# Moving loads, stores and PSUM copies in a two-layer recurrent trunk (GLA, S5, mLSTM) on one core

## The chip, the cores and the metric

The kernel runs on one core of one Trainium2 chip. The metric is the device time of one execution in microseconds (us); lower is better. The time before is the median of three runs.

## What is computed

One inference step of a two-layer trunk, for a prompt of 256 tokens and for 8 samples of 8 tokens each (320 tokens, d_model 2048). Each of four sub-layers applies RMSNorm, a shift and scale from the condition vector (adaLN), its mixer or its SwiGLU feed-forward, and a gated residual add:

```python
def gla_mix(...):      # layer 0, 4 heads: S_t = diag(a_t) S_{t-1} + k_t^T v_t,  o_t = q_t S_t
def s5_mix(...):       # layer 0, 64 groups of 16 channels, each a 64-dim complex diagonal state (associative scan)
def mlstm_mix(...):    # layer 1, 4 heads: C_t = f_t C_{t-1} + i_t v_t k_t^T, n_t likewise, m_t a running maximum
...
x = x + gate * mixer(modulate(x, c, ...));  x = x + gate * swiglu(modulate(x, c, ...))
```

The outputs are the normed tokens of both groups and the final states: of GLA (128 x 256 for each head and sample), of S5, and of mLSTM (C of 512 x 256 for each head and sample, 512 KB; n; m).

## The kernel before

All large products are y = W^T x with the weights as the stationary operand in 128 x 128 tiles and the 320 tokens as the moving columns. Full precision comes from splitting both operands into a rounded part and a rest (`hi`, `lo` of the weights, `xh`, `xl` of the activations) and adding three products. Weights come in units of 512 KB on SyncE's (SP's) queue; ScalarE (ACT) makes `hi` by a cast, VectorE (DVE) makes `lo` by a subtraction, six half units ahead of the products (`split_to`, L590; `run_pair`, L604).

All else runs as generators (tasks) between these products. The kernel is written out once, in the order of a planner (`Est`, L130): a cost model with one clock for each engine, for SP and for the DMA engines. A task yields the tensors that it needs next; after every three products `tick` (L383) resumes the tasks whose tensors the model believes ready. What comes out is one fixed order of instructions for each engine, so an edit of a task shifts the order of all that comes after it. Each engine runs its own instructions in order, waiting on semaphores, and two engines that read the same PSUM bank wait for each other. When nothing else is ready, a filler product is emitted (`warm`, L389) or a step of the adaLN products (`ada`), which fill in between.

The order of the stages: conditions and first norm; input projection, with S5 and GLA as tasks; output projection; feed-forward 0; mLSTM projections with `ml_task`; output projection; feed-forward 1; last norm and output.

The places that the change touches:

- S5, `apply1` (L1178): for each of 8 blocks and each of two parts (`ri`), products into one bank, then a copy of 64 x 4 columns by ScalarE and one of 16 x 4 columns by VectorE out of that bank.
- S5, `toep` (L1297): for each of 8 blocks, 16 copies of 32 partitions out of one bank, in four groups (`i`) of four (`t`). The groups alternate between VectorE and ScalarE. `apply2` (L1310) multiplies by what they write.
- GLA, `gla_tail` (L1645), one for each head: a sample's new state is the product of masked keys `KM` (96 x 128) with values, and a DVE update of `S`. `km(b)` (L1664) makes the masked keys on GpSimd (POOL); the loop yields once for each of the 8 samples.
- mLSTM, `ml_gates` (L1933): the gate rows of all four heads in partitions 0 to 3 of `rows_b` (`Mr`, `er`, `gi`). At its end it loads the state n (`nr`), waits for it, transposes it and sets the flag "gates", for which `ml_task` waits.
- mLSTM, `ml_task` (L2066): for each head three products spread a row of `rows_b` over all 128 partitions (L2093 to L2100, below); `sel` is 1 in row h and 0 in all other rows. Then, for each of 8 samples (step g = 8 h + b), C lies in one of three buffers `CR`. The order of a step is: yield for C and for `EV`; `old(b - 1)`; `store(g - 1)` on SP; eight transposes of C; yield; products; two DVE updates of C in place; `load_c(g + 2)` on SP, into the buffer that `store(g - 1)` reads.
- `ml_begin` (L2292) opens the stage's memory and loads the constants. `z1_end` (L2337) waits for the flag "nout", which `ml_task` sets at its end, before the output projection begins.

```python
mm(ps[:, 0:T], sel[0:4, h, :], ML["er"])
act.copy(eb, ps[:, 0:T])
mm(ps[:, T:T + 64], sel[0:4, h, :], ML["gi"])
act.copy(gb, ps[:, T:T + 64])
```

In the profile every instruction has the line of one helper (L220), so instructions are told apart by their tiles: `misc` are the small PSUM banks, `mm` the large ones, `ada` the adaLN bank; `S_slab`, `G_slab`, `GR_slab` and `R_slab` are the memories of S5, GLA, GLA's masked keys and mLSTM; `fix_slab` holds weights and constants.

Of the kernel before, what the change touches and what calls it, by code (L numbers as in the profile page):

```python
# [16 lines left out]
AF = mybir.ActivationFunctionType  # L17
# [216 lines left out]
def trunk(tc, a, o, coff, dbg=None, stop=None):  # L234
# [5 lines left out]
    with (  # L240
# [66 lines left out]
        def con(name):  # L307
            f, n = coff[name]
            return cst[0].v(n, o=f) if f < NC1 else cst[1].v(n, o=f - NC1)
# [30 lines left out]
        def f(ap):  # L340
            return ap.bitcast(F32)
# [786 lines left out]
        def s5_task():  # L1128
# [49 lines left out]
            def apply1(j):  # L1178
                U4 = U4_b.v(4, 81, o=324 * (j % 3))
                M1 = M1_b[j % 2].v(8, P)  # L1180
                pr4 = slice(4 * j, 4 * j + 4)
                for ri in range(2):
                    ps = mps()
                    for i in range(4):
                        mm(ps[:, 81 * i:81 * i + 81], M1[:, 4 * ri + i, :], U4[:, i, :])
                    pv = ps[:, 0:324].rearrange("p (q c) -> p c q", q=4)
                    act.copy(H[:, 1:65, ri, pr4], pv[:, 0:64, :])
                    vec.tensor_copy(H[:, 73:89, ri, pr4], pv[:, 65:81, :])

            done1, done2 = [0, 0], [0, 0]  # L1190
            build1(0)
# [105 lines left out]
            def toep(j):  # L1297
                WBf, TT = WB_b.v(2, 4, 160, o=1280 * (j % 2)), TT_b.v(4, P, o=512 * (j % 2))
                ps = yield from kept()
                for ri in range(2):  # L1300
                    for i in range(4):
                        mm(ps[32 * i:32 * i + 32, 0:P], BB[:, ri, i, :], WBf[:, ri, i, 0:P], ri == 0, ri == 1)
                yield [ps]
                for i in range(4):
                    for t in range(4):
                        (act.copy if i % 2 else vec.tensor_copy)(TT[32 * t:32 * t + 32, i, 32 * t:P],
                                                                 ps[32 * i:32 * i + 32, 0:P - 32 * t])
                drop(ps[:, :])

            def apply2(j):  # L1310
# [144 lines left out]
        def gla_task():  # L1455
# [9 lines left out]
            for h in range(4):  # L1465
# [103 lines left out]
                for g in range(2):  # L1569
                    sp.dma_start(out=S[:, 4 * g:4 * g + 4, :],  # L1570
                                 in_=a["state_gla"][0, 4 * g:4 * g + 4, h].rearrange("b k v -> k b v"))
                kt_b, km_b = alG(3 * P + 16, top=True), M["GR"].get(512)
                kh_b = alG(T + 64)
                kh, qh = kh_b.v(T), kh_b.v(64, o=T)
                kt, bl = kt_b.v(3, P), kt_b.v(16, o=3 * P)
# [69 lines left out]
        def gla_tail(h, S_b, kt_b, km_b, v_b):  # L1645
# [1 line left out]
            S, kt, bl, vt = S_b.v(NB, 256), kt_b.v(3, P), kt_b.v(16, o=3 * P), v_b.v(3, 256)  # L1647


            VS, KS, KM = km_b.v(256), f(km_b.v(P, o=256)), km_b.v(P, o=384)  # L1650
            kr = km_b.v(P, o=256)

            def stack(x):
# [9 lines left out]

            def km(b):  # L1664

                pool.tensor_scalar(KM[0:96], KS[0:96], con("sb4")[0:96, b % 4:b % 4 + 1], None, MUL)

            yield [kt, vt]
            stack(0)
# [4 lines left out]
            so = stage()[:, 0:256]  # L1674
            act.copy(so, ps[:, 0:256])
            act.dma_start(out=o[2][0, 0, h], in_=so)
            for b in range(NB):
                if b == 4:
                    stack(1)
                if b:  # L1680
                    km(b)
                yield [VS, KM, S]
                ps = mps()
                mm(ps[:, 0:256], KM[0:96], VS[0:96])
                vec.scalar_tensor_tensor(S[:, b, :], S[:, b, :], bl[:, b:b + 1], ps[:, 0:256], MUL, ADD)
            yield [S]
            sp.dma_start(out=o[8][0, :, h].rearrange("b k v -> k b v"), in_=S)
            for b in (S_b, kt_b, km_b, v_b):
# [236 lines left out]
        def alM(n):  # L1925
            return M["R"].get(n)
# [6 lines left out]
        def ml_gates(zb):  # L1933
# [82 lines left out]
            nr = ML["n_b"].v(256, o=136)  # L2016
            nT = ML["nT"] = ML["n_b"].v(2, 32)
            ML["nn"] = ML["n_b"].v(2, 36, o=64)
            sp.dma_start(out=nr[0:32], in_=a["state_mlstm_n"][0].rearrange("b h d -> (b h) d"))
            yield [nr]  # L2020
            ps = mps()
            for i in range(2):
# [43 lines left out]
        def ml_task():  # L2066
# [18 lines left out]
            for h in range(4):  # L2085
# [5 lines left out]
                bc_b = alM(2 * T + 64)  # L2091
                Mb, eb, gb = bc_b.v(T), bc_b.v(T, o=T), bc_b.v(64, o=2 * T)
                ps = mps()  # L2093
                mm(ps[:, 0:T], sel[0:4, h, :], ML["Mr"])
                act.copy(Mb, ps[:, 0:T])
                ps = mps()
                mm(ps[:, 0:T], sel[0:4, h, :], ML["er"])
                act.copy(eb, ps[:, 0:T])
                mm(ps[:, T:T + 64], sel[0:4, h, :], ML["gi"])
                act.copy(gb, ps[:, T:T + 64])  # L2100

                wk_b = alM(4 * T)
                w, wS = wk_b.v(3 * P), wk_b.v(64, o=3 * P)
# [112 lines left out]
                for b in range(NB):  # L2216
# [4 lines left out]
                    yield [C, EV]  # L2221
                    if b:
                        old(b - 1)
                        store(g - 1)
                    for d in range(2):
                        ps = mps()
                        for c in range(4):
# [11 lines left out]
                    for c2 in range(2):  # L2239
                        ps = mps()  # L2240
                        for c1 in range(2):
                            c = 2 * c2 + c1
                            mm(ps[:, 256 * c1:256 * c1 + 256], VS[0:96, b // 4, c * P:(c + 1) * P], km)
                        vec.scalar_tensor_tensor(C[:, 2 * c2:2 * c2 + 2, :], C[:, 2 * c2:2 * c2 + 2, :], dec[:, h, b:b + 1],
                                                 ps.rearrange("p (a b) -> p a b", a=2), MUL, ADD)
                    load_c(g + 2)
                yield [EV, C]
                old(7)
                store(8 * h + 7)

                for c in range(4):
                    vec.tensor_mul(hh[:, c, TP:T], hh[:, c, TP:T], rd[:, TP:T])
# [39 lines left out]
        def ml_begin():  # L2292
# [11 lines left out]
            cst[1] = alM(NC2)  # L2304
            sp.dma_start(out=cst[1].v(NC2), in_=a["consts"][:, NC1:NC1 + NC2])
            ML.update(rows_b=alM(2 * T + 64 + 16), tok_b=alM(3 * 8 + 32 + 4 * 27), n_b=alM(64 + 2 * 36 + 256 + 16))
            for h in range(2):
                ML["v", h], ML["q", h], ML["k", h] = alM(3 * 512), alM(2 * T), alM(2 * T)
            ML["vs"] = M["L"].get(4 * T)
# [179 lines left out]
```

## Time and profile before

| | us |
|---|---|
| median of three runs | 3345.41 |
| lowest, highest | 3341.87, 3347.14 |
| the profiled execution, its own time | 3340.73 |
| its span, first to last instruction | 3338.9 |
| mean granted TensorE clock | 0.987 |

The profile is of one execution. A row of grouped instructions has its busy time, the mean of one, and the idle time of the engine just before them with what ended it. In a timeline the idle time and what ended it stand in brackets. A granted clock of 1.00 is 2.4 GHz and 0.50 is 1.2 GHz; a value in between is a stretch that had both.

### The profile page before, as it was taken

The page shows a single profiled execution, that of the slowest core. Times are in us where ns is not written, and L with a number is a line of the kernel's source. Part 1 is how long each engine was busy: PE and PEld are TensorE (multiplying, and loading weights), DVE is VectorE, ACT ScalarE, POOL GpSimd, SP SyncE. Part 2 cuts the span into 40 slices and gives each one's busy share as a digit, 9 for nine tenths or more (in the row PEclk, how much of TensorE's full clock was granted, in tenths as well). Part 3 has the DMA queues.
Part 4 walks back from the last instruction along what each step waited for, and adds up shares of the span by engine and source line. Part 5 has one row for each costly group of instructions (what it writes and reads, how often), then busy time and mean ns, then how long its engine had stood idle before and what let it go on. Part 6 is the DMA issues. An engine that isn't in the chain of part 4 may idle for free.

```text
span 3338.9 us, 57434 instructions
## 1 busy us (share of the span) xinstructions
PE 3247.1 (97%) x22658; PEld 3024.8 (91%) x22658; DVE 1857.3 (56%) x3842; ACT 1312.6 (39%) x2479; POOL 335.0 (10%) x508
## 2 busy tenths in 40 slices
PE   7898999999999999999999999999999999999998
PEld 4687788889899898999998999999999999999997
DVE  3768777764444444444474665566645545544546
ACT  3354454343333333333433343344443343343343
POOL 0225411320000000000040000002200000000002
PEclk9999899999999999999999999999999999999999
DMA  9887688677676776765454664565444444444443
GB/s 309 295 271 250 195 301 321 230 271 254 241 275 236 269 248 246 271 239 196 149 170 135 196 202 136 174 198 198 148 152 149 149 151 152 146 152 152 151 148 100
DMA packets 536350, 686.63 MB, mean 206 GB/s; under 512 B 41096, under 2 KB 495056, under 8 KB 515024
## 3 DMA queue, kind: packets, MB, share of 16 engines
q1 hardware_dynamic: 533024, 680.26, 61.1%
q8 instruction: 178, 2.92, 0.4%
q10 hardware_dynamic: 3056, 2.70, 0.2%
q14 instruction: 92, 0.75, 0.1%
HBM read 643.19 MB, written 39.69 MB: 205 GB/s over the span
## 4 chain that ended last, share of the span: by engine, by line
PE 85%; DVE 5%; DMA 4%; ACT 2%; POOL 1%; issue 1%; SPq 0%; ACTq 0%; DVEq 0%; POOLq 0%
PE mm L220 74%; PE misc L220 8%; PE ada L220 4%; DVE lo L220 1%; DVE X_slab L220 1%; POOL S_slab L220 1%; DMA fix_slab<-in_ab_ada_w_dram 1%; DVE S_slab L220 1%; DVE G_slab L220 1%; DVE xl L220 1%; DMA out_dram<-R_slab 1%; DMA R_slab<-in_state_mlstm_C_dram 0%; ACT S_slab L220 0%; ACT hi L220 0%; ACT xh L220 0%
## 5 line engine op out<-in xcount | busy, mean ns | idle before, releaser
L220 DVE TENSOR_TENSOR lo<-fix_slab,hi 128x512 fp32r<-128x512 f32 (+1 forms) x1556 | 1089.9, 706 | 1168.7 <-ACT hi L220 1164.6
L220 ACT CAST hi<-fix_slab 128x512 fp32r<-128x512 f32 (+1 forms) x1556 | 946.1, 613 | 1427.7 <-PE mm L220 1372.4
L220 PE MATMUL mm<-xh,hi 128*128 128x320 f32 x4704 | 1481.4, 315 | 10.8 <-DVE S_slab L220 7.5
L220 PE MATMUL mm<-xl,hi 128*128 128x320 f32 x4704 | 1460.6, 311 | 0.6 <-DVE xl L220 0.6
L220 PE MATMUL mm<-xh,lo 128*128 128x320 f32 x4704 | 1459.7, 310 | 0.9 <-DVE lo L220 0.9
L220 PEld LDWEIGHTS mm<-xh,hi 128*128 128x128 f32 x4704 | 889.6, 189 | 56.8 <-issue 30.4
L220 PEld LDWEIGHTS mm<-xh,lo 128*128 128x128 f32 x4704 | 890.0, 189 | 2.1 <-DVE lo L220 1.6
L220 PEld LDWEIGHTS mm<-xl,hi 128*128 128x128 f32 x4704 | 888.6, 189 | 2.6 <-DVE xl L220 2.6
L220 PE MATMUL mm<-ffh,hi 128*128 128x320 f32 x1408 | 435.8, 309 | 0.0
L220 PE MATMUL mm<-ffh,lo 128*128 128x320 f32 x1408 | 434.4, 308 | 0.0
L220 PE MATMUL mm<-ffl,hi 128*128 128x320 f32 x1408 | 434.3, 308 | 0.0
L220 POOL TENSOR_TENSOR X_slab<-X_slab 128x320 f32<-128x320 f32 (+1 forms) x117 | 109.7, 938 | 2019.0 <-DVE X_slab L220 1985.9
L220 PEld LDWEIGHTS mm<-ffh,hi 128*128 128x128 f32 x1408 | 264.0, 187 | 6.7 <-issue 6.7
L220 PEld LDWEIGHTS mm<-ffh,lo 128*128 128x128 f32 x1408 | 264.0, 188 | 0.0
L220 PEld LDWEIGHTS mm<-ffl,hi 128*128 128x128 f32 x1408 | 264.0, 187 | 0.0
L220 PE MATMUL ada<-fix_slab 128*32 128x512 f32 x952 | 122.8, 621 | 8.1 <-DMA fix_slab<-in_ab_ada_w_dram 8.1
L220 POOL TENSOR_TENSOR S_slab<-S_slab 128x32 f32<-128x32 f32 (+3 forms) x226 | 114.8, 517 | 88.9 <-ACT S_slab L220 41.3
L220 DVE SCALAR_TENSOR_TENSOR ffs<-ffs,mm 128x320 f32<-128x320 f32 x176 | 81.6, 488 | 26.7 <-ACT ffs L220 22.9
L220 DVE SCALAR_TENSOR_TENSOR X_slab<-mm,fix_slab,X_slab 128x256 f32<-128x256 f32 x176 | 84.6, 480 | 11.3 <-PE mm L220 11.3
L220 PEld LDWEIGHTS ada<-fix_slab 128*32 128x32 f32 x952 | 25.3, 111 | 58.9 <-issue 49.1
L220 DVE TENSOR_TENSOR S_slab<-S_slab 128x256 f32<-128x256 f32 (+3 forms) x167 | 70.4, 433 | 7.2 <-POOL S_slab L220 3.1
L220 PEld LDWEIGHTS misc<-S_slab 128*128 128x128 f32 (+1 forms) x448 | 47.7, 187 | 20.0 <-issue 11.6
(154 smaller groups left out, 1833.3 us busy)
## 6 DMA issues: line engine op xcount, KB each, us to landing
fix_slab<-in_ffn_w_dram SPq DMA_DIRECT2D x524, 512.0 KB, 3.4
fix_slab<-in_ffn_ada_w_dram SPq DMA_DIRECT2D x65, 1024.0 KB, 7.8
fix_slab<-in_ml_w_in_dram SPq DMA_DIRECT2D x96, 512.0 KB, 4.5
fix_slab<-in_ab_ada_w_dram SPq DMA_DIRECT2D x35, 1024.0 KB, 7.4
fix_slab<-in_ab_w_in_dram SPq DMA_DIRECT2D x64, 512.0 KB, 7.3
adam<-in_ffn_ada_w_dram SPq DMA_DIRECT2D x31, 1024.0 KB, 9.4
adam<-in_ml_ada_w_dram SPq DMA_DIRECT2D x29, 1024.0 KB, 8.0
fix_slab<-in_ml_ada_w_dram SPq DMA_DIRECT2D x19, 1024.0 KB, 8.4
```

What stands on the lines that cost most here:

```text
L220: r = call(*a, **k)
```

## The change

- `apply1`: both copies of a bank are made by one engine, ScalarE for the first part, VectorE for the second.
- `toep`: all 16 copies are made by ScalarE.
- `gla_tail`: samples go in pairs. ScalarE makes both masked keys (an activation with a scale per partition) in place of GpSimd; two products go into one bank, then two updates; four yields in place of eight. `km_b` grows from 512 to 640 columns.
- mLSTM: the load of n moves from `ml_gates` to `ml_begin`. `rows_b` is set to zero there by GpSimd, and the spread products run over all 128 rows. The second and third go into one bank without a copy between, and one copy takes both.
- mLSTM: `store(g)` comes at the end of its own step, behind a new yield for C, just ahead of `load_c(g + 2)`; the last store comes ahead of `old(7)`.

```diff
@@ apply1
-                    act.copy(H[:, 1:65, ri, pr4], pv[:, 0:64, :])
-                    vec.tensor_copy(H[:, 73:89, ri, pr4], pv[:, 65:81, :])
+                    copy = vec.tensor_copy if ri else act.copy
+                    copy(H[:, 1:65, ri, pr4], pv[:, 0:64, :])
+                    copy(H[:, 73:89, ri, pr4], pv[:, 65:81, :])
@@ toep
-                        (act.copy if i % 2 else vec.tensor_copy)(TT[32 * t:32 * t + 32, i, 32 * t:P],
-                                                                 ps[32 * i:32 * i + 32, 0:P - 32 * t])
+                        act.copy(TT[32 * t:32 * t + 32, i, 32 * t:P], ps[32 * i:32 * i + 32, 0:P - 32 * t])
@@ gla_task
-                kt_b, km_b = alG(3 * P + 16, top=True), M["GR"].get(512)
+                kt_b, km_b = alG(3 * P + 16, top=True), M["GR"].get(640)
@@ gla_tail
-            VS, KS, KM = km_b.v(256), f(km_b.v(P, o=256)), km_b.v(P, o=384)
+            VS, KS, KM = km_b.v(256), f(km_b.v(P, o=256)), km_b.v(2, P, o=384)
...
-                pool.tensor_scalar(KM[0:96], KS[0:96], con("sb4")[0:96, b % 4:b % 4 + 1], None, MUL)
+                for i in range(2):
+                    x = (b + i) % 4
+                    act.activation(KM[0:96, i, :], KS[0:96], AF.Copy, scale=con("sb4")[0:96, x:x + 1])
...
-            for b in range(NB):
+            for b in range(0, NB, 2):
...
-                mm(ps[:, 0:256], KM[0:96], VS[0:96])
-                vec.scalar_tensor_tensor(S[:, b, :], S[:, b, :], bl[:, b:b + 1], ps[:, 0:256], MUL, ADD)
+                for i in range(2):
+                    mm(ps[:, 256 * i:256 * i + 256], KM[0:96, i, :], VS[0:96])
+                for i in range(2):
+                    vec.scalar_tensor_tensor(S[:, b + i, :], S[:, b + i, :], bl[:, b + i:b + i + 1],
+                                             ps[:, 256 * i:256 * i + 256], MUL, ADD)
@@ ml_gates
-            sp.dma_start(out=nr[0:32], in_=a["state_mlstm_n"][0].rearrange("b h d -> (b h) d"))
             yield [nr]
@@ ml_task, head of a head
-                mm(ps[:, 0:T], sel[0:4, h, :], ML["Mr"])
+                mm(ps[:, 0:T], sel[:, h, :], ML["rows_b"].v(T))
                 act.copy(Mb, ps[:, 0:T])
                 ps = mps()
-                mm(ps[:, 0:T], sel[0:4, h, :], ML["er"])
-                act.copy(eb, ps[:, 0:T])
-                mm(ps[:, T:T + 64], sel[0:4, h, :], ML["gi"])
-                act.copy(gb, ps[:, T:T + 64])
+                mm(ps[:, 0:T], sel[:, h, :], ML["rows_b"].v(T, o=T))
+                mm(ps[:, T:T + 64], sel[:, h, :], ML["rows_b"].v(64, o=2 * T))
+                act.copy(bc_b.v(T + 64, o=T), ps[:, 0:T + 64])
@@ ml_task, loop over samples
                         old(b - 1)
-                        store(g - 1)
...
+                    yield [C]
+                    store(g)
                     load_c(g + 2)
-                yield [EV, C]
+                yield [EV]
                 old(7)
-                store(8 * h + 7)
@@ ml_begin
+            sp.dma_start(out=ML["n_b"].v(256, o=136)[0:32], in_=a["state_mlstm_n"][0].rearrange("b h d -> (b h) d"))
+
+            pool.memset(ML["rows_b"].v(2 * T + 64), 0.0)
```

## Rows read from the trace of the kernel before

**Rows 1.** The page, part 1: busy us, share of the span, instructions.

```profile
PE 3247.1 (97%) x22658; PEld 3024.8 (91%) x22658; DVE 1857.3 (56%) x3842; ACT 1312.6 (39%) x2479; POOL 335.0 (10%) x508
```

**Rows 2.** Windows: length; busy of PE, PEld, DVE, ACT, POOL; clock; DMA share; GB/s.

```profile
318.00:342.00 24.00, 16.45 (x98) 13.63 (x97) 15.92 (x46) 10.67 (x31) 12.38 (x31) 0.64 0.64 208
342.00:362.00 20.00, 16.85 (x118) 14.69 (x117) 15.17 (x41) 9.19 (x29) 16.71 (x48) 0.83 0.48 156
...
398.00:630.00 232.00, 225.50 (x1633) 191.08 (x1626) 164.04 (x467) 112.53 (x271) 38.96 (x58) 1.00 0.83 290
```

**Rows 3.** Waits of PE, 1743 to 2260 us: total us, times, longest.

```profile
PE misc L220 <- DMA R_slab<-in_state_mlstm_C_dram: 3.8, 4, 1.8
PE misc L220 <- DMA R_slab<-in_state_mlstm_n_dram: 3.0, 1, 3.0
PE misc L220 <- ACT R_slab L220: 2.1, 4, 0.5
```

**Rows 4.** Timeline at the n state: start us, us, engine, operation.

```profile
1784.81 0.42 PE L220 MATMUL misc<-fix_slab,R_slab 32*128 32x32 f32 x2 [3.05 <-DMA R_slab<-in_state_mlstm_n_dram]
```

**Rows 5.** Windows of the mLSTM stage, columns as in rows 2.

```profile
1784.00:1796.00 12.00, 10.68 (x40) 8.72 (x40) 2.58 (x9) 2.58 (x7) 1.06 (x3) 0.57 0.49 164
1900.00:1904.00 4.00, 4.00 (x21) 3.96 (x19) 2.18 (x8) 1.18 (x3) 0.99 (x3) 0.57 0.02 4
...
2100.00:2104.00 4.00, 2.22 (x18) 1.98 (x17) 0.88 (x2) 0.66 (x2) 0.00 (x0) 1.00 0.80 223
```

**Rows 6.** Timeline of head 1's spread products on PE.

```profile
1897.24 1.34 PE L220 MATMUL misc<-R_slab 4*128 4x320 f32 x4
...
1899.10 0.43 PE L220 MATMUL misc<-R_slab 4*128 4x64 f32 x2 [0.52 <-ACT R_slab L220]
```

**Rows 7.** The chain in order of time: start us, us, what.

```profile
1908.24 3.18 PE misc L220 x22
```

**Rows 8.** Waits of SP's queue, 1743 to 2260 us: total us, times, longest.

```profile
SPq L220 <- DMA out_dram<-R_slab: 144.7, 28, 6.5
```

**Rows 9.** DMA issues: count, KB each, median us from issue to landing.

```profile
R_slab<-in_state_mlstm_C_dram SPq DMA_DIRECT2D x32, 512.0 KB, 4.1
out_dram<-R_slab SPq DMA_DIRECT2D x32, 512.0 KB, 6.3
```

**Rows 10.** Timeline of SP in head 1: stores of C.

```profile
1951.00 0.46 SPq L220 DMA_DIRECT2D out_dram<-R_slab  x1
...
1958.46 0.50 SPq L220 DMA_DIRECT2D out_dram<-R_slab  x1
```

**Rows 11.** Timeline of ACT in head 1: EV, once a step.

```profile
1938.46 0.27 ACT L220 COPY fix_slab<-misc 128x128 f32<-128x128 f32 x1 [1.99 <-PE misc L220]
...
1942.94 0.27 ACT L220 COPY fix_slab<-misc 128x128 f32<-128x128 f32 x1 [0.48 <-PE misc L220]
```

**Rows 12.** Timeline of one S5 block: products, copies, the products behind them.

```profile
348.16 0.62 PE L220 MATMUL misc<-S_slab 128*32 128x128 f32 x16
...
351.28 0.90 ACT L220 COPY S_slab<-misc 32x128 f32<-32x128 f32 x4 [4.95 <-DVE S_slab L220]
...
353.24 0.91 ACT L220 COPY S_slab<-misc 32x128 f32<-32x128 f32 x4 [1.06 <-DVE S_slab L220]
...
354.20 5.41 PE L220 MATMUL misc<-S_slab 128*128 128x81 f32 x24 [2.69 <-ACT S_slab L220]
```

**Rows 13.** Waits of PE, 216 to 630 us: total us, times, longest.

```profile
PE misc L220 <- DVE G_slab L220: 8.2, 3, 5.7
...
PE misc L220 <- POOL GR_slab L220: 2.7, 6, 0.8
```

**Rows 14.** Groups by form: busy us, mean ns, idle before.

```profile
L220 POOL TENSOR_SCALAR GR_slab<-GR_slab,fix_slab 96x128 fp32r<-96x128 f32 x32 | 24.4, 762 | 131.2 <-ACT GR_slab L220 35.6 <-PE misc L220 25.1 <-ACT G_slab L220 21.2
...
L220 ACT CAST GR_slab<-G_slab 32x128 fp32r<-32x128 f32 x16 | 4.7, 295 | 0.1
```

**Rows 15.** Timeline of PE where the output projection begins.

```profile
2254.58 0.49 PE L220 MATMUL misc<-fix_slab 128*128 128x128 f32 x2
```

## The prediction

> **What bounds the kernel now.** The page's busy shares come first: TensorE is busy 97% of the span, the other engines 56% or less [rows 1]. So time is saved only where TensorE stands idle, where its granted clock is down, or where it computes less. The change takes no product away, so I looked for idle time and lost clock in the stretches that it touches. The windows by stage give both: idle is the length less PE busy, and lost clock is the length times one minus the granted clock. S5 and GLA, from the first changed copy (about 219 us) to 630 us, have two bad stretches: 318 to 342 us with 7.6 us idle and 24 x 0.36 = 8.6 us of clock lost, and 342 to 362 us with 3.2 and 3.4 us. From 398 us to 630 us 6.5 us are idle and no clock is lost [rows 2]. In the mLSTM stage (1743 to 2260 us) TensorE's waits are three: C tiles from memory 3.8 us, the n state 3.0 us, ScalarE's copies of the spread rows 2.1 us [rows 3]. Next to these stands the clock, read from windows at those waits [rows 5]. Everything before 219 us is the same program, and the feed-forward stages are not touched.
>
> **The n state.** Its load moves from the gates task to the opening of the stage, ahead of the gate products. Now TensorE waits 3.05 us for it at 1781.8 us [rows 4], and the clock is at 0.57 over the following 12 us [rows 5]: 12 x 0.43 = 5.2 us. Both go: 8.2 us. SP now issues it behind a constants load, one issue among weight loads; what it is moved past (two small stores, two weight loads) doesn't wait for it. The added memset of 704 columns is on GpSimd, which has nothing to do there; at the price of a GpSimd operation of the tail (0.76 us for 128 columns, [rows 14]) it stays under 5 us, and what it must precede are the gate rows, which come only after the gate products, two scans and exponentials. Cost nothing; a reader that came at once would cost those 5 us.
>
> **Spread products.** Per head, two products with 4 rows take 1.34 us, TensorE waits 0.52 us for ScalarE's copy out of the bank it must write, and a third product follows with 0.43 us [rows 6]. Then the clock falls: 0.57 over 4 us in head 1 [rows 5], and the two later heads show the same pattern. That is 4 x 0.43 = 1.7 us each, 5.1 us for three heads (head 0's is in the 12 us above). After: the third product follows the second with no copy between, which takes the 2.1 us of [rows 3]; and all products run over 128 rows, whose time goes by columns. Does the clock then stay? An idle time of 1.78 us at 2101.5 us left it at 1.00 [rows 5], and so did 22 products of full height that filled 3.18 us from 1908.24 us [rows 7]. So what fell short in the spread is most likely the 4-row products: with the wait they make 2.3 us. I take the whole 5.1 us; the other end is nothing.
>
> The Trainium skill ("TensorE: Matmul & The Clock Gate", Part 4) says that transposes don't count as TensorE work in the way that products do. Transposes stand right behind the spread here, so by that sentence they could be what lowers the clock; it is the third rival below.
>
> **C tiles.** One buffer of three is stored, then loaded again. Now SP waits for the store's end before it can issue the load behind it: 144.7 us in 28 waits [rows 8], a store of 6.3 us and then a load of 4.1 us [rows 9], with stores 7.46 us apart [rows 10]. After: the store is issued one step earlier, and the load waits for the store of the step before, which is over when steps are longer than 6.3 us. Weight loads behind it on SP come earlier too. Added is a wait: the store needs VectorE's update of C, and on SP the C load and weight loads queue behind it; the planner yields on that update first, so I cost it at nothing (other end: a 1.4 us update for 32 steps, on SP, which has 144.7 us to give back). Of the 3.8 us that TensorE waits for C, I take 3; the ends are 3.8 gained, and a loss that is the first rival.
>
> **S5's copies.** In one block, products that end at 348.78 us are copied by four groups of four in turn, VectorE, ScalarE, VectorE, ScalarE. Each engine waits for the other, and both queues are held meanwhile; ScalarE starts only at 351.28 us, after 4.95 us idle, its last group ends at 354.15 us, and TensorE waits 2.69 us for it [rows 12]. After: ScalarE, idle, starts near 349.0 us and needs 16 x 0.225 = 3.6 us (four take 0.90): it ends at 352.6 us, 1.5 us sooner. The rest of the wait (1.2 us) is shorter than the 1.78 us that cost no clock, so the 3.4 us of clock in that stretch go too: 4.9 us. VectorE is free of some 3 us a block (two groups and the wait between). That acts inside the stretch from 318 us on, where TensorE waits 5.7 us for VectorE's reading of a bank, the longest of three waits of 8.2 us in all [rows 13]: 3 us gained, with the clock left as it is (ends: 0, and 5.7 + 8.6). The other blocks: 1 us. Eight blocks give ScalarE some 8 x 1.8 = 14 us more in 230 us; its queue holds the weight casts, but it was held in the same places by VectorE. The copies after the first S5 product change engine in pairs, one bank each, off TensorE's path: nothing.
>
> In the Trainium skill ("PSUM — Partial Sum Buffer", the rule under bank collisions) different 32-partition quadrants of a bank may be read together. These groups read one quadrant each, so by that rule two engines could share a block and finish in about 1.9 us. The trace shows them taking turns, because the program guards whole banks; with that guard one engine is the quicker.
>
> **GLA tail.** GpSimd's 32 masked keys of 0.76 us become 32 on ScalarE, at about 0.30 us by the cast of the same width [rows 14]: 9.5 us over four tails, beside casts that themselves wait for TensorE. TensorE's 2.7 us of waits for GpSimd [rows 13] go, say 2. ScalarE now waits for the previous pair's products before it overwrites the keys, with weight casts behind it, and VectorE and TensorE behind those; it is placed where those casts wait for TensorE too, so nothing. Without that cover 16 waits of up to 0.5 us would cost 8 us.
>
> **The sum.** mLSTM: 8.2 + 2.1 + 5.1 + 3 = 18.4 us. S5 and GLA: 4.9 + 3 + 1 + 2 = 10.9 us. Together 29.3 us. Against the profiled execution, 3340.7 us, it gives 3311.4 us; the median of the three runs lies 4.7 us above that execution, so **3316 us**.
>
> **Rivals.**
> 1. Slower, by one mechanism: in the C loop a load is now queued right behind its own 512 KB store. If it lands as late as a store does (6.3 us, [rows 9]) and the plan runs steps as fast as the first ones, 4.48 us apart [rows 11], each of the later 24 steps stalls 1.8 us: 43 us, against the other 26 us gained: 3362 us. It decides where the step is shorter than the load's landing. Against: steps are 7.46 us apart now [rows 10], a load alone lands in 4.1 us, and an added yield lengthens the step. 6%.
> 2. Another planning of S5 and GLA. The kernel orders its instructions by estimated times, so all after 219 us is ordered anew, and a new stall like that at 318 us (16 us with its clock) can come where the old one went. Then that part gives from -4 to 0: 3327 to 3331 us. For: the waits there hang on details of order. Against: the new order has fewer hand-overs between engines. 16%.
> 3. The clock falls in heads 1 to 3 all the same, because of transposes or short products: 5.1 us stay, 3321 us. Against: steps of the C loop hold eight transposes each, and the window at 2100 us, with one such step and idle time, keeps 1.00 [rows 5]. 10%.
> 4. The stall at 318 us goes wholly, with its clock: 11 us more, 3305 us or, with the rest of [rows 2], 3299 us. 10%.
> 5. The mLSTM loop gets longer: it ends just as the next stage needs it (one filler product at 2254.58 us, [rows 15]), so a longer last head moves TensorE's end: with the yield at 1 us, eight steps make 8 us, 3324 us. Against: the step's length is now set by store and load, which overlap afterwards. 5%.
>
> **How the numbers follow.** The forecast's own case (3308 to 3322 us) has about 50%. The remaining 3% are an edit without effect, near 3342 us. From 3299 us (the fourth rival) to 3337 us (the second, with 6 us for the added waits that I cost at nothing) some 8 in 10 lie inside. A difference of 0.2%, 6.7 us, is about what a measurement of this kernel can tell from none, so faster means under 3338.7 us. Same: those 3% and a quarter of the second rival, 0.07; slower: the first, 0.06; faster: the rest, 0.87.
>
> **What would show it.** Right: no wait for the n state, and granted clock 1.00 in the 12 us behind it and behind each head's spread; no ScalarE wait between spread products; SP's wait for stores far below 144.7 us; S5's copies in groups of 16 on ScalarE, with no wait of it for VectorE; no GpSimd in the tail. Wrong: a clock of 0.5 behind the spread (rival 3), C waits of over 10 us (rival 1), or idle time between 219 and 630 us that is not below today's.

## The result

| | before, us | after, us |
|---|---|---|
| median | 3346.27 (4 runs) | 3305.32 (4 runs) |
| lowest, highest | 3341.87, 3347.55 | 3301.39, 3311.96 |
| profiled execution, its span | 3340.73, 3338.9 | 3311.96, 3310.2 |
| mean granted clock | 0.987 | 0.990 |

The ratio is 0.988 with a 95% interval of 0.986 to 0.990: 1.2% faster, some 41 us. The profiled execution of before lies 5.5 us under its median, that of after is the slowest of its four, 6.6 us over its median: so the two profiles are 28.8 us apart, and what follows by stages accounts for these and not for all 41 us. A second profile of after (span 3302.4 us) stands among the experiments.

**Where the time went.** The long pieces of the chain of work are the same in both kernels, so their starts cut the span into stages. The lines of after, with start, length and what it is (the first stands near the start of the work, the second is a long run of products behind S5 and GLA, the third opens mLSTM, the fourth is feed-forward 1):

```profile
56.13 3.71 PE mm L220 x24
...
624.75 50.14 PE mm L220 x340
...
1734.68 18.38 PE mm L220 x113
...
2365.60 866.56 PE mm L220 x5898
```

and of before:

```profile
52.15 3.71 PE mm L220 x24
...
633.11 50.14 PE mm L220 x340
...
1743.41 18.33 PE mm L220 x113
...
2394.66 866.57 PE mm L220 x5898
```

The lead of after is 8.4 us behind S5 and GLA, still 8.7 us where mLSTM opens, and 29.1 us at feed-forward 1. After reached the first of these pieces 4.0 us later than before; nothing is changed in front of it, and in its second profile it came at 52.77 us. So from that first piece on, S5 and GLA gave 581.0 - 568.6 = 12.4 us, and mLSTM 651.25 - 630.92 = 20.3 us. The rest is equal.

**mLSTM.** Windows over the whole stage (columns: window, its length, PE busy, PEld, DVE, ACT, POOL busy, granted clock, DMA share, GB/s), before:

```profile
1743.41:2394.66 651.25, 639.16 (x4645) 601.92 (x4646) 395.19 (x829) 262.40 (x512) 72.16 (x82) 0.98 0.57 175
```

and after:

```profile
1734.68:2365.60 630.92, 626.86 (x4645) 596.47 (x4646) 395.95 (x829) 261.57 (x508) 72.82 (x83) 0.99 0.60 181
```

The same 4645 products: 8.0 us less idle time (12.1 to 4.1) and 12.3 us less busy time. Windows of 2 us over the stage, each with its length times one minus the granted clock, put 8.5 us of that down to the clock: before lost 11.9 us (1.7 at the opening of the stage, 5.1 in head 0, 1.7 behind the spread of each later head), after 3.4 us (1.7 at the opening, 1.7 in head 2). The other 3.8 us are busy time at full clock, nearly all in heads 1 to 3, and nothing here tells what they were. The 12 us behind head 0's spread in after:

```profile
1771.23:1783.23 12.00, 12.00 (x83) 11.34 (x83) 8.30 (x20) 2.91 (x6) 4.29 (x7) 1.00 0.62 197
```

What TensorE and SP waited for in it (total us, times, longest), after:

```profile
PE misc L220 <- DVE X_slab L220: 2.4, 1, 2.4
PE mm L220 <- DVE lo L220: 0.9, 1, 0.9
PE misc L220 <- DVE lo L220: 0.8, 1, 0.8
PE misc L220 <- DMA R_slab<-in_state_mlstm_C_dram: 0.8, 1, 0.8
...
SPq L220 <- DVE R_slab L220: 68.2, 37, 5.1
...
SPq L220 <- DMA out_dram<-R_slab: 5.2, 2, 4.4
```

Of [rows 3] the wait for n and those for ScalarE are gone, and of the C tiles' 3.8 us 0.8 is left. SP's 144.7 us for the stores [rows 8] are 5.2 us; in their place it waits 68 us for VectorE's updates (11.7 us before), and TensorE's waits for C tiles fell all the same.

**S5 and GLA.** The windows of [rows 2], and one between them, after:

```profile
318.00:342.00 24.00, 22.61 (x172) 18.77 (x165) 18.08 (x35) 9.61 (x23) 10.96 (x22) 1.00 0.62 200
342.00:362.00 20.00, 19.72 (x141) 17.20 (x141) 12.43 (x37) 15.83 (x52) 13.46 (x34) 0.74 0.74 244
362.00:398.00 36.00, 31.86 (x225) 25.49 (x225) 27.83 (x63) 18.92 (x59) 20.59 (x38) 0.86 0.72 253
398.00:630.00 232.00, 227.28 (x1645) 196.19 (x1646) 158.75 (x448) 126.97 (x328) 21.86 (x36) 0.99 0.82 290
```

The third of these windows in before, and its wait for ScalarE there that [rows 13] leaves out:

```profile
362.00:398.00 36.00, 33.61 (x236) 27.40 (x238) 29.18 (x75) 15.39 (x38) 10.77 (x15) 0.91 0.71 225
...
PE misc L220 <- ACT S_slab L220: 7.3, 7, 2.7
```

TensorE's longest waits in after, to be held against [rows 13]:

```profile
PE misc L220 <- DVE S_slab L220: 4.4, 3, 3.5
PE misc L220 <- DVE fix_slab L220: 2.5, 2, 1.4
PE misc L220 <- DVE G_slab L220: 2.2, 4, 0.8
```

The stall at 318 us is gone with its clock, and of the 7.3 us of waits for ScalarE 0.3 is left; but 342 to 398 us now loses 20 x 0.26 + 36 x 0.14 = 10.2 us of clock, where before lost 20 x 0.17 + 36 x 0.09 = 6.6 us, and there is a new wait of 3.5 us. The waits for GpSimd went with the tail.

### The profile page after: what moved, and what is told of

Same layout as the page of the kernel before. It is cut to its first block, busy times and chain, and to the rows that moved or that the text cites. A ratio compares the mean times of both kernels' runs of the same rounds, so it can differ in the third digit from the quotient of the medians.

```text
span 3310.2 us, 57482 instructions
## 1 busy us (share of the span) xinstructions
PE 3240.2 (98%) x22678; PEld 3027.2 (91%) x22678; DVE 1840.3 (56%) x3778; ACT 1331.5 (40%) x2571; POOL 314.0 (9%) x477
## 4 chain that ended last, share of the span: by engine, by line
PE 90%; DVE 4%; DMA 3%; ACT 2%; issue 1%; POOL 0%; SPq 0%; ACTq 0%; DVEq 0%; POOLq 0%
PE mm L220 77%; PE misc L220 8%; PE ada L220 5%; DVE lo L220 1%; DVE X_slab L220 1%; DMA fix_slab<-in_ab_ada_w_dram 1%; DVE S_slab L220 1%; ACT hi L220 0%; DMA fix_slab<-in_ab_w_in_dram 0%; DVE G_slab L220 0%; DVE xl L220 0%; SPq L220 0%; POOL S_slab L220 0%; ACT S_slab L220 0%; DMA S_slab<-in_x_sample_dram 0%
## 5 line engine op out<-in xcount | busy, mean ns | idle before, releaser
L220 ACT CAST ffh<-ffs 128x320 fp32r<-128x320 f32 x88 | 39.6, 460 | 57.5 <-DVE ffs L220 57.5
```

The lines of the kernel that those rows point to most:

```text
L220: r = call(*a, **k)
```

## The experiments

Two theories. Mine: each part gives what its wait and the clock behind it are worth, and the parts add up. The rivals: the clock falls at some short product or other whatever is done about the spread, and S5 and GLA's time is set by the order that the planner finds. Stage lengths in us, each from one profile (S5 and GLA from the chain's first `mm` piece of 24 to that of 340; mLSTM to feed-forward 1), and the time against before, run beside it on the same chip:

| kernel | S5 and GLA | mLSTM | ratio, 95% interval | clock | rest |
|---|---|---|---|---|---|
| before | 581.0 | 651.3 | | | |
| n load alone | 579.1 | 646.3 | 0.9993 (0.9981 to 1.0005) | 1.3 | 1.4 |
| spread alone | 579.0 | 644.0 | 0.9974 (0.9962 to 0.9985) | 3.5 | 4.0 |
| store order alone | 579.4 | 644.5 | 0.9982 (0.9973 to 0.9991) | 1.0 | 4.9 |
| S5's copies alone | 587.1 | 659.3 | 1.0020 (1.0010 to 1.0030) | 5.1 | -12.7 |
| GLA tail alone | 589.2 | 652.9 | 1.0023 (1.0010 to 1.0035) | -5.7 | -2.4 |
| 128 rows, old copies | 578.0 | 650.0 | 0.9994 (0.9981 to 1.0006) | 1.5 | -0.1 |
| 4 rows, merged copy | 578.1 | 649.5 | 0.9999 (0.9988 to 1.0010) | -0.9 | 0.2 |
| after | 568.6 | 630.9 | 0.9882 (0.9863 to 0.9901) | | |
| after, again | 564.2 | 630.2 | 0.9906 (0.9886 to 0.9926) | 11.6 | 17.9 |
| old order, new copies | 566.7 | | 0.9954 (0.9939 to 0.9969) | 10.4 | 4.9 |
| after's order, old copies | 588.0 | 636.8 | 0.9957 (0.9941 to 0.9974) | 0.4 | 12.1 |
| after, another fill bound | | 634.3 | 0.9903 (0.9888 to 0.9918) | 13.1 | 19.3 |
| all but the GLA tail, old order | 570.8 | 633.3 | 0.9892 (0.9876 to 0.9908) | 15.2 | 20.0 |

(A cell is empty where the chain is cut at another place, or where no clock of before is on record beside the runs.) The last two columns split the gain over all runs, in us: every run has its mean granted clock on record, its time multiplied by one minus that clock is what the clock took from it, and the rest is what would be left at full clock. The means are good to some 2 to 5 us either way (95%).

Kernels with the same S5 and GLA lie between 578.0 and 581.0 us there, those with the old mLSTM between 651.3 and 659.3 us and with the new one between 630.2 and 636.8: a single profile tells a few us in S5 and GLA, not in mLSTM. The single edits of mLSTM are therefore judged by all their runs.

**The n load alone**, out of `ml_gates` into `ml_begin`.

```diff
-            sp.dma_start(out=nr[0:32], in_=a["state_mlstm_n"][0].rearrange("b h d -> (b h) d"))
...
+            sp.dma_start(out=ML["n_b"].v(256, o=136)[0:32], in_=a["state_mlstm_n"][0].rearrange("b h d -> (b h) d"))
```

> Only the load of the n state is moved ahead of head 0's block. By the prediction's terms PE's wait of 3.05 us for n at 1784.81 goes and the clock of 1784 to 1796, granted at 0.57, stays up: 5.2 us more, 8.2 us in all, about 3332.5 in a run like the profiled one. The rival is that head 0's own spread (three products on four rows and the 0.52 us gaps between them) lowers the clock whatever n does: then the wait alone goes and the fall stands at head 0's spread, 3 us in all. The whole in the mLSTM stage, nothing elsewhere.

The wait is gone, and the stage is 4.9 us shorter in this profile; over all runs the time lies between 6 us gained and 2 us lost, which leaves out my 8.2 us and holds the rival's 3. The clock behaves as neither theory said. Windows over head 0's spread (its first copy at 1781.11 us):

```profile
1779.11:1783.11 4.00, 3.48 (x16) 2.46 (x16) 3.25 (x19) 1.69 (x4) 0.00 (x0) 0.90 0.52 133
1783.11:1787.11 4.00, 4.00 (x23) 3.89 (x22) 1.85 (x7) 1.03 (x3) 0.37 (x1) 0.67 0.36 23
1787.11:1791.11 4.00, 4.00 (x29) 3.71 (x28) 2.44 (x5) 0.78 (x2) 1.54 (x4) 1.00 0.88 228
```

It lost 4 x 0.10 + 4 x 0.33 = 1.7 us here, as at each later head, in place of 5.2 us. So head 0 hides two causes, the wait and the spread, and both must go for its whole loss to go.

**The spread alone, and its two halves.** All of it, with both edits (here and in the first half the first spread product runs on 128 rows too, and `rows_b` is set to zero, as in the change):

```diff
-                mm(ps[:, 0:T], sel[0:4, h, :], ML["er"])
-                act.copy(eb, ps[:, 0:T])
-                mm(ps[:, T:T + 64], sel[0:4, h, :], ML["gi"])
-                act.copy(gb, ps[:, T:T + 64])
+                mm(ps[:, 0:T], sel[:, h, :], ML["rows_b"].v(T, o=T))
+                mm(ps[:, T:T + 64], sel[:, h, :], ML["rows_b"].v(64, o=2 * T))
+                act.copy(bc_b.v(T + 64, o=T), ps[:, 0:T + 64])
```

> Only the spread is changed: products on 128 rows and two copies merged into one. By the prediction 2.1 us of idle time in four heads and 5.1 us of lost clock in heads 1 to 3 go, 7.2 us in all; head 0 still waits 3.05 us for n and still falls to 0.57 after it. If the transposes and short products around the spread lower the clock, not its four rows and its gap, the 0.57 windows after 1900 stay and it gives 2.1 us.

One half: 128 rows, but the copies as before.

```diff
-                mm(ps[:, 0:T], sel[0:4, h, :], ML["er"])
+                mm(ps[:, 0:T], sel[:, h, :], ML["rows_b"].v(T, o=T))
                 act.copy(eb, ps[:, 0:T])
-                mm(ps[:, T:T + 64], sel[0:4, h, :], ML["gi"])
+                mm(ps[:, T:T + 64], sel[:, h, :], ML["rows_b"].v(64, o=2 * T))
                 act.copy(gb, ps[:, T:T + 64])
```

> Only the rows of the spread products: 128 in place of four, the copy between the second and the third product stays. If the four rows lower the clock, the 0.57 windows of heads 1 to 3 rise to 1.00 and 5 us are gained, with the waits of 0.52 us still there. If the gap or the transposes lower it, the windows stay at 0.57 and nothing is gained.

The other half: four rows, but one copy of 384 columns.

```diff
                 mm(ps[:, 0:T], sel[0:4, h, :], ML["er"])
-                act.copy(eb, ps[:, 0:T])
                 mm(ps[:, T:T + 64], sel[0:4, h, :], ML["gi"])
-                act.copy(gb, ps[:, T:T + 64])
+                act.copy(bc_b.v(T + 64, o=T), ps[:, 0:T + 64])
```

> Only the merged copy: the products keep four rows, the wait of 0.52 us between the second and the third goes. If the four rows lower the clock, it stays at 0.57 in heads 1 to 3 and 2.1 us are gained. If the gap lowers it, the windows rise to 1.00 and 7 us are gained.

Together they gained 7.2 us in the stage of this profile, and 5 to 13 us over all runs, which holds the forecast of 7.2 us: 3.5 us of clock and 4.0 us of the rest, where the forecast had 5.1 and 2.1. Each half alone gained nothing that can be told from zero, though in the first the window behind head 1's spread stood at 1.00, with a wait of 0.51 us still there:

```profile
1899.33:1903.33 4.00, 4.00 (x29) 3.89 (x28) 2.45 (x8) 1.70 (x4) 1.30 (x3) 1.00 0.01 4
...
2010.01:2018.01 8.00, 8.00 (x46) 7.92 (x46) 5.21 (x9) 1.24 (x2) 2.72 (x3) 0.79 0.15 37
```

The second line is why: in head 2 the clock fell 10 us later. So does it in the second half's kernel, in all three heads, for instance in head 1:

```profile
1897.63:1901.63 4.00, 4.00 (x26) 3.40 (x25) 1.79 (x5) 1.52 (x3) 0.00 (x0) 1.00 0.68 239
1909.63:1917.63 8.00, 8.00 (x47) 7.93 (x47) 4.88 (x10) 1.99 (x4) 2.72 (x3) 0.79 0.22 63
```

Counted over heads 1 to 3 of every profile, by windows of 4 us:

| spread | profiles | falls right behind it | falls some 10 us later |
|---|---|---|---|
| four rows, copy between | 6 | 10 of 18 | 1 of 18 |
| 128 rows, copy between | 1 | 0 of 3 | 1 of 3 |
| four rows, merged copy | 1 | 0 of 3 | 3 of 3 |
| 128 rows, merged copy | 6 | 0 of 18 | 9 of 18 |

With either half or both taken away the clock fell right behind the spread in 0 of 24 heads, with the old spread in 10 of 18. For both together that stands on six profiles against six. For one half alone it stands on a single profile, and two of the six profiles with the old spread (the GLA tail alone; the old order with the new copies) show no such fall either: whether one half is enough is not shown. Where both are taken away, the clock falls some 10 us later in half of the heads. In the profile of after that is head 2 (start, length, instruction):

```profile
1989.77 1.77 PE L220 MATMUL misc<-R_slab,fix_slab 128*128 128x256 f32 x10
1991.37 1.74 PE L220 MATMUL misc<-R_slab 128*128 128x9 f32 x12
1993.04 0.42 PE L220 MATMUL mm<-xh,hi 128*128 128x320 f32 x1
...
1994.36 0.47 PE L220 MATMUL mm<-xl,hi 128*128 128x320 f32 x1
```

Twelve products of 9 columns, and 1.1 us behind them the products go from 0.31 to 0.47 us. Before, they stood there too ([rows 7] ends with them) without a fall. And the old spread did not always lower the clock: with the old order and the new copies of S5, whose TensorE instructions are those of before in the same order from first to last, all three windows of 4 us behind the spread show 1.00, for instance

```profile
1890.83:1894.83 4.00, 4.00 (x29) 3.92 (x28) 2.32 (x8) 1.71 (x4) 1.17 (x3) 1.00 0.02 6
```

The same instructions in the same order, with a fall in one profile and none in another. So it is with the late falls: after, after again and after's order with the old copies have one TensorE order, and show one, none and three. Nor does the fall simply move on: in the eight heads where the old spread passed at full clock, the thin products passed too. What else decides it is open.

**The store order alone.**

```diff
-                        store(g - 1)
...
+                    yield [C]
+                    store(g)
                     load_c(g + 2)
```

> Only the order of the loop over the C tiles: each tile's store is issued in its own step behind the copy, and the load of the tile two ahead right behind that store. By the prediction SP's 144.7 us of waiting for the stores falls to some us, PE's 3.8 us of waiting for C tiles go to below 1, and the kernel gains 3 us. The rival is that the load now stands behind its own tile's store on SP and lands late: up to 0.7 us in each of 31 steps, 22 us slower. No change of the clock either way.

```profile
PE misc L220 <- DMA R_slab<-in_state_mlstm_C_dram: 0.6, 1, 0.6
...
SPq L220 <- DMA out_dram<-R_slab: 2.5, 2, 1.6
```

TensorE's waits for C tiles went from 3.8 to 0.6 us, SP's for the stores to 2.5 us, and the idle time of the stage from 12.1 to 9.1 us: the 3 us of the forecast. Over all runs the edit gave 3 to 9 us. The first rival (loads late behind their own stores) didn't come.

**S5's copies alone, and the GLA tail alone.** The main lines of each; the rest of `apply1` and of the tail is as in the change.

```diff
-                        (act.copy if i % 2 else vec.tensor_copy)(TT[32 * t:32 * t + 32, i, 32 * t:P],
-                                                                 ps[32 * i:32 * i + 32, 0:P - 32 * t])
+                        act.copy(TT[32 * t:32 * t + 32, i, 32 * t:P], ps[32 * i:32 * i + 32, 0:P - 32 * t])
```

> Only S5's copies: the block of toep copied by ScalarE alone and each bank of apply by one engine. By the prediction the waits of 2.69 us for ScalarE between the toep blocks at 348 to 362 go down and 4.9 us of 342 to 362 come back, with some 3 us more where VectorE is freed of its half: 5 to 9 us faster. If ScalarE takes the four copies of a block one after the other at the same 0.5 us each, a block takes as long as before and the gain is 0 to 2 us. If the planner puts other work there, the stretch from 318 to 398 is moved by some us either way and the clock in it decides.

```diff
-                pool.tensor_scalar(KM[0:96], KS[0:96], con("sb4")[0:96, b % 4:b % 4 + 1], None, MUL)
+                for i in range(2):
+                    x = (b + i) % 4
+                    act.activation(KM[0:96, i, :], KS[0:96], AF.Copy, scale=con("sb4")[0:96, x:x + 1])
...
-            for b in range(NB):
+            for b in range(0, NB, 2):
```

> Only the tail of GLA: two samples in a step, the masked keys on ScalarE in place of POOL. By the prediction POOL's 32 products of 762 ns and PE's 2.7 us of waits for them go and ScalarE takes 32 short copies: 2 us faster (0 to 5). If ScalarE is late in S5 beside it, waits of PE for ScalarE of some 8 us come in their place, in 216 to 398. The prediction did not make the GLA tail end the 7.6 us stall at 318; if it does, this kernel alone shows it, at 9 us faster.

Both are slower than before, by 7 and 8 us over all runs and 6.1 and 8.2 us in S5 and GLA, where together they are 12 to 17 us faster. No sum of parts gives that; the order must be in it. In the first, the stall of 5.7 us is gone, and TensorE's idle time in the stage (43.1 to 40.5 us) and its lost clock (22.1 to 18.7 us, by windows of 2 us) both went down; it is longer because TensorE has more to do in it (below). In the second TensorE waits 8.9 us for ScalarE, once 5.9 us:

```profile
PE misc L220 <- ACT S_slab L220: 8.9, 5, 5.9
```

**The order held, the copies changed, and the other way round.** The planner is a model that is told of each instruction, so it can be told of others than those that run. First the new copies in the order of before:

```diff
-                        (act.copy if i % 2 else vec.tensor_copy)(TT[32 * t:32 * t + 32, i, 32 * t:P],
-                                                                 ps[32 * i:32 * i + 32, 0:P - 32 * t])
+                        x = TT[32 * t:32 * t + 32, i, 32 * t:P], ps[32 * i:32 * i + 32, 0:P - 32 * t]
+                        nc.scalar.copy(*x)
+                        est.note(*(("ACT", "copy") if i % 2 else ("DVE", "tensor_copy")), x, {})
```

(and `apply1` in the same way)

> S5's copies as the change makes them, but the planner is told of the old ones, so that the order of the instructions is that of the kernel before on every engine, with the copies on the other engine. By the working on the block of toep the freed VectorE and the shorter block give 5 to 8 us, the 7.6 us idle at 318 goes down with VectorE's load, and the order has no part in it. By the rival (the time of S5 and GLA is set by the order that the planner finds) the stretch stays within 2 us of the kernel before, and the stall at 318 stands.

Then the old copies in the order of after:

```diff
-                        act.copy(TT[32 * t:32 * t + 32, i, 32 * t:P], ps[32 * i:32 * i + 32, 0:P - 32 * t])
+                        x = TT[32 * t:32 * t + 32, i, 32 * t:P], ps[32 * i:32 * i + 32, 0:P - 32 * t]
+                        (nc.scalar.copy if i % 2 else nc.vector.tensor_copy)(*x)
+                        est.note("ACT", "copy", x, {})
```

(and `apply1` in the same way)

> The changed kernel with its own order of instructions, but S5's copies on the chip are the old ones (toep by both engines in turn, each bank of apply by two): the planner is told of the new ones. If the new copies themselves save the time, S5 and GLA go back by 5 to 8 us against the changed kernel. If the order saves it, the stretch stays within 2 us of the changed kernel, some 15 us shorter than before, and the stall at 318 stays away.

The copies have the gain: 14.2 us in the stage and 14.4 us in the median with the old order (3342.77 to 3328.34 us), and 19 to 24 us in the order of after. In both orders most of it is clock (10.4 us in the old order; 11.6 against 0.4 us in that of after). But the order has a price of the same size. S5's copies alone, and the same copies in the old order, run the same instructions on VectorE, ScalarE and GpSimd in S5 and GLA; windows over the stage of the first:

```profile
54.53:641.61 587.08, 546.61 (x3868) 457.82 (x3868) 394.42 (x1023) 276.14 (x672) 162.77 (x305) 0.97 0.79 266
```

and of the second:

```profile
54.15:620.89 566.74, 531.69 (x3793) 448.93 (x3793) 393.50 (x1023) 278.00 (x672) 163.22 (x305) 0.97 0.81 277
```

VectorE's 1023, ScalarE's 672 and GpSimd's 305 instructions are the same; TensorE has 75 more in the stage, which is 20.3 us longer. All but one of the 75 are filler products. Their group in the stage (count, busy us, mean ns) in before, in S5's copies alone, in the GLA tail alone and in after:

```profile
L220 PE MATMUL misc<-fix_slab 128*128 128x128 f32 x54 | 8.4, 276 | 0.4 <-DVE fix_slab L220 0.4
...
L220 PE MATMUL misc<-fix_slab 128*128 128x128 f32 x128 | 20.3, 287 | 0.7 <-DVE G_slab L220 0.2
...
L220 PE MATMUL misc<-fix_slab 128*128 128x128 f32 x104 | 14.8, 280 | 0.0
...
L220 PE MATMUL misc<-fix_slab 128*128 128x128 f32 x74 | 11.1, 284 | 0.0
```

In the old order with the new copies it is that of before. So what differs is the planner's order and the fillers that come with it: 20.3 - 8.4 = 11.9 us of the 20.3 us are fillers, 5.4 us are idle time. Whether the fillers took the time, or stand in waits that this order would have had anyway, no run tells.

One block of the copies, first VectorE's first group in before (its others are in [rows 12]), then the old order with the new copies (ScalarE, and the products that wait for it):

```profile
350.23 0.96 DVE L220 COPY S_slab<-misc 32x128 f32<-32x128 f32 x4
...
347.33 3.66 ACT L1310 COPY S_slab<-misc 32x128 f32<-32x128 f32 x16 [2.69 <-PE misc L220]
...
351.04 0.34 PE L220 MATMUL misc<-S_slab 128*128 128x81 f32 x1 [1.05 <-ACT S_slab L1310]
```

ScalarE starts when the bank is written, not after VectorE, and TensorE waits 1.05 us where it waited 2.69 us in the same place [rows 12]. (3.66 / 16 is 0.23 us a copy, not the 0.5 us that the expectation for S5's copies alone set against the forecast.) The 28 us around the stall, then the 56 us behind it, each first in before and then here:

```profile
312.00:340.00 28.00, 20.45 (x126) 17.63 (x125) 19.82 (x46) 11.24 (x30) 14.74 (x31) 0.70 0.76 256
314.00:342.00 28.00, 24.15 (x161) 21.44 (x154) 20.71 (x44) 18.59 (x55) 18.51 (x41) 0.82 0.75 268
...
342.00:398.00 56.00, 50.46 (x352) 42.10 (x354) 44.35 (x115) 24.59 (x67) 27.48 (x62) 0.88 0.63 200
344.00:400.00 56.00, 53.91 (x430) 45.27 (x433) 41.91 (x103) 34.68 (x112) 28.86 (x57) 0.97 0.77 257
```

**All but the GLA tail.** The changed kernel with the tail of before, and S5's copies noted as above:

```diff
-                for i in range(2):
-                    x = (b + i) % 4
-                    act.activation(KM[0:96, i, :], KS[0:96], AF.Copy, scale=con("sb4")[0:96, x:x + 1])
+                pool.tensor_scalar(KM[0:96], KS[0:96], con("sb4")[0:96, b % 4:b % 4 + 1], None, MUL)
```

> All of the change but the tail of GLA, which stays as it was, and S5 and GLA's instructions in the order of the kernel before (the planner is told of the old copies). If the gains of the parts add up and the tail of GLA has none of its own, the copies of S5 give 14.4 us and the mLSTM edits some 20: about 3308, as fast as the changed kernel. If the tail of GLA carries a part of the changed kernel's gain, this one is slower than that by so much (2 us by the prediction).

3305.91 us, ratio 0.9892: as fast as after (0.9882 and 0.9906). The parts add up once the order of S5 and GLA is held (n load, spread, store order and copies gave 2 + 9 + 6 + 15 = 32 us over all their runs, this kernel 31 to 41 us), and the tail has no gain of its own that these runs, which can't tell 2 us, show.

**The changed kernel again, and with another bound for fillers.**

> The changed kernel once more, for a second profile of it. If what it lost of the clock at 342 to 398 (granted 0.74 and 0.86) belongs to its order of instructions, the same stretch has it again, to within a microsecond. If it belongs to the run, this profile shows another clock there and a span some us shorter. The same question for head 2 of mLSTM, whose window behind the score products stood at 0.57.

The loss behind 342 us came again, in the same stretch (from the same start of the chain, 338.64 to 358.64 us, and the 36 us behind it), a little smaller:

```profile
338.64:358.64 20.00, 19.16 (x149) 16.75 (x149) 13.97 (x42) 16.13 (x58) 16.32 (x43) 0.85 0.75 268
358.64:394.64 36.00, 31.51 (x222) 25.32 (x222) 26.66 (x60) 19.20 (x60) 18.87 (x30) 0.87 0.69 230
```

That is 20 x 0.15 + 36 x 0.13 = 7.7 us. So a loss there belongs to after's order, but of the 10.2 and 7.7 us only 3.6 and 1.1 are more than the 6.6 us that before lost in 342 to 398 us. The fall in head 2 of mLSTM did not come again: that one belongs to the run.

```diff
-        FILL, WARM, OWN, CHK = 1.9, 1, 0, 1
+        FILL, WARM, OWN, CHK = 1.5, 1, 0, 1
```

> The changed kernel with one constant of the planner changed (an idle stretch of PE is filled with a pending product of the adaLN weights from 1.5 us on, not from 1.9): the order changes behind S5 and GLA alone. If idle time there is on the path, it gives up to 2 us; if the products only move from a later place, nothing. It is also a look at how much of S5 and GLA's time moves from one profile to the next with the same order there.

3311.05 us (ratio 0.9903): no gain over the changed kernel.

## Why the prediction was right

3305 us lies in the range, 11 us below the forecast of 3316 us. The sum, 29.3 us, is close to what the two profiles are apart (28.8 us) and a little under what the sets of runs gave: 41 and 31 us for after, 32 us with another fill bound, 36 us without the GLA tail. By kind it is close too: the sum holds 5.2 + 5.1 + 3.4 = 13.7 us of clock and 15.6 us of idle time, and the last three of these sets give 11.6 to 15.2 us of clock and 17.9 to 20.0 us of the rest. But two of its terms were off in opposite ways, and that they made up for each other is luck. Step by step:

- **n state** (8.2 us forecast): right as a wait, too simple as a clock. Alone the move left a fall of 1.7 us to the spread, and over all runs it gave 1.3 us of clock and 1.4 us of the rest. With both gone, the 12 us behind head 0's spread are at 1.00 in after, so the 8.2 us came, but with two edits as their cause.
- **Spread, idle time** (2.1 us): gone, as [rows 3] said.
- **Spread, clock of heads 1 to 3** (5.1 us): the step that failed. I read from [rows 5 to 7] that the four rows made the fall in every head, and that without them the clock stays. The runs show that the old spread had the fall in 10 of 18 heads, and that without it the fall comes at the thin products in 9 of 18. At 1.7 us a fall, and with the old spread's one late fall counted too, that is (11 - 9) / 6 x 1.7 = 0.6 us for a kernel by this count, not 5.1; before, with all three heads fallen, and after with one, happened to show 3.4. Six profiles with none to three falls each don't fix the size closely, and over all runs the spread alone gave 3.5 us of clock in the whole kernel, good to some 3 us: how large the term is stays open, but the clock does not stay up as I had it. The third rival (short products) had the better reason. Its rule from the Trainium skill ("TensorE: Matmul & The Clock Gate", Part 4: transposes don't count as TensorE work in the way that products do) is not borne out as the cause by itself here: the transposes behind the spread are the same in all these kernels, and in the 24 heads where either half was changed no clock fell right behind them.
- **C tiles** (3 us): 3.0 us of idle time when alone, and the waits fell from 3.8 to 0.6 us. All runs together put it at 3 to 9 us.
- **mLSTM in sum** (18.4 us): 20.3 us between the two profiles, 8.0 us idle, 8.5 us clock and 3.8 us in neither. The idle terms, 3.05 + 2.1 + 3 = 8.2 us, fit. Of the clock term, 5.2 + 5.1 = 10.3 us, head 0's part came whole; the 3.4 us of heads 1 to 3 owe their size to the run in which before was profiled.
- **S5's copies** (4.9 + 3 + 1 = 8.9 us): right in kind, too small: 14.4 us (10 to 20 over all runs) with TensorE's order unchanged. The term that failed is the clock. I had 3.4 us of it and 5.5 us of idle time; the runs give 10.4 and 4.9 us. The freed VectorE was put at 3 us "with the clock left as it is": in the 28 us around the stall the idle time went down by 3.7 us, and the lost clock by 28 x 0.12 = 3.4 us with it. The 56 us behind it gave 3.5 us of idle time and 56 x 0.09 = 5.0 us of clock, where I had 5.9 us in all.
- **GLA tail** (2 us): none that can be told.
- **The order** (second rival, 16%, some 11 to 15 us lost): it came in both parts alone. In S5's copies it cost some 22 us (ratios of 1.0020 and 0.9954 for the same copies); for the GLA tail no run holds the order. That it did not come with all parts together is not something my argument had shown. The fourth rival came by half: the stall went wholly, but behind it, where I had 3.4 us of clock come back, 1.1 to 3.6 us more went lost.

What stays open is why the planner's order is good with both edits and bad with each. The fillers go with it (54 before, 128 and 104 with one edit, 74 with both), but they may be the cause or only the sign. Open too is the fall of the clock at one short product or the next, which comes in one run and not in another with the same instructions.

## What to carry to other kernels

When a planner writes the order, an edit has two prices: its work, and the order that it brings. Hold the order (tell the planner of the old instructions) to see the first; here it is 14 us faster where the edit by itself came out 7 us slower. Count the planner's fillers too: they keep TensorE busy, so a longer order doesn't show as idle time. A clock that falls behind one short run of products in one profile may fall behind another, or nowhere, in the next, so count such falls over several profiles before they go into a sum.

## What was not expected of the hardware

Two engines that take turns at one bank, as this program has them do, held both queues: 16 copies by one engine took 3.66 us, about as long as by two in turn (350.23 to 354.15 us, 3.9 us), and yet S5's copies were worth 14 us, most of it clock. And the granted clock fell (0.57 over 1994 to 1998 us of after) in stretches in which TensorE was never idle, behind 12 products of 9 columns, in 9 of 18 heads of the changed spread.
